# Gates and ups kept by column tile, block products of 256 columns, and the step-size projection in four column groups

## The chip, the cores and the metric

The kernel runs on one core of one Trainium2 chip. TensorE (PE in the profile) multiplies matrices, VectorE (DVE) and ScalarE (ACT) do the elementwise work, GpSimd (POOL) issues a few transfers that add into their destination, and SyncE (SP) issues the other transfers. PEld is TensorE's loading of weights. The metric is the device time of one execution, in microseconds (us), as the median of several runs.

## The reference

The model is an encoder of two layers on one sequence of 512 frames with 1024 channels, in float32. Each layer is a half-weighted SwiGLU, a mixer, and another half-weighted SwiGLU, each on a normalised input and added to x:

```python
def _swiglu(h, w_gate, w_up, w_down):
    return (jax.nn.silu(h @ w_gate) * (h @ w_up)) @ w_down
...
        h = _rmsnorm(x, ffn1_norm[layer])
        x = x + 0.5 * _swiglu(h, ffn1_w_gate[layer], ffn1_w_up[layer], ffn1_w_down[layer])
        h = _rmsnorm(x, mix_norm[layer])
        if layer % 2 == 0:
            proj = h @ even_w_in[i]
            zxbcdt, u = jnp.split(proj, [SSD_INNER + SSD_XBC + SSD_HEADS], axis=-1)
            y_a = _ssd_mixer(zxbcdt, ssd_conv_w[i], ssd_conv_b[i], ssd_dt_bias[i],
                             ssd_a_log[i], ssd_d[i], ssd_norm[i])
...
```

The hidden width of a SwiGLU is 2816, that is 22 column tiles of 128, or 11 pairs of tiles. In the state-space half (SSD) of the even mixer eight columns of the input projection give the step sizes, dt = softplus(dt + dt_bias), and the decay is the running sum of dt * (-exp(a_log)).

## The kernel before

Activations lie transposed: 128 channels on the partitions, 512 frames along the free axis; so a projection of one column tile is a matmul of 512 columns (frames) for each of 8 channel tiles. Float32 is emulated: each operand is split into a rounded high part and a low rest (ScalarE casts the high part, VectorE subtracts to get the low one), and three matmuls (high by high, high by low, low by high) take the place of one. The tiles whl and wh hold split weights, hg split activations, raw weights as they arrive.

The stages follow one another: f0 (a SwiGLU, about 0 to 379 us), the even mixer (to 560), f1 and f2 (to 904 and 1255), the odd mixer (to 1434) and f3. In a SwiGLU the first column pairs are done plainly (8 of 11 in f0, 2 of 11 in f1 to f3, the table CLASSIC): proj_tile() makes one tile, evac() scales it out of PSUM (rsB is the norm's factor, applied late), gate() applies Silu, multiplies gate by up and splits the result into hg. The other column pairs are done by pair() with seven block products in place of eight (a scheme of Strassen's kind, on blocks of 512 channels by 128 columns of weights and 256 frames): feed() builds sums of weight blocks on VectorE, blocks() sums of activation blocks, block() does a product of four 128-channel steps, and plus(), add and times gather the seven results from PSUM on VectorE. pair() leaves its last product to be done in the next one (last, called as before). With WIDE set, the three products that take one of the summed activation tiles (TA, TB) send the high and low halves of the activation through as one matmul of 512 columns, whose two halves of PSUM plus() then adds with two additions; without it they send two matmuls of 256 columns into the same half, and one addition does.

The down-projections (out_unit) run between the pairs, also in plain matmuls of 512 columns. Most raw weights are split by ScalarE and VectorE; those that BY_DMA names are split by split_dma(): ScalarE writes the negated high part and POOL's transfer adds the raw weights from memory to it.

A planner orders the instructions of TensorE, VectorE and ScalarE while the program is built: Clock estimates when each engine and tile is ready, and generators (threads, with priorities PRIO) wait in on() until their inputs will be ready by the main stream's own time plus a margin (SLACK for TensorE; BACKLOG and GUARD bound how far VectorE and ScalarE may be filled ahead). Each engine then runs its list in that order. In the even mixer, ssd_dt() turns the step sizes into dt and the decays, s5_bounce() and s5_eighth() carry the S5 half through memory (us, s5us, s5ys, parameter tiles prm), and ssd_chunk() and ssd_tail() do the SSD half. The transfers of all of these go through SyncE's one queue, in the order in which they are written. The step-size columns are the first projection of the even mixer: proj_tile(wdt, m=8), 24 matmuls whose output is 8 partitions wide. Norm sums (sq, acc, then ones by acc on TensorE) are gathered beside the last down-projections. Nearly every instruction is recorded through one helper, so the profile gives them all one line, 223 (226 in the changed kernel); groups are told apart by tiles.

## Time and profile before

| | |
|---|---|
| median of 3 runs | 1810.75 us (1807.51 to 1813.69) |
| the profiled execution | 1812.46 us, span 1810.8 us |
| TensorE busy | 1787.6 us, 99% of the span, granted clock 0.998 |
| VectorE busy | 1518.0 us, 84% |
| ScalarE busy | 744.5 us, 41% |
| POOL busy | 33.9 us, 2% |
| bytes moved | 216.57 MB, mean 120 GB/s |

A row of a group gives the line, engine, operation, output and inputs by tile name, their shapes and count; then the busy time in us, the mean length of one in ns, and the idle time of the engine just before them with what ended it. A row of a timeline gives start and length in us, the engine and the operation, how many of one kind ran in a row (x), and in brackets the idle time before it and what released it. A row of the chain of waits gives a start and a length on the path that ended last. A row of busy time by stretch gives, after the stretch and its length, the busy us (and instructions) of PE, PEld, DVE, ACT and POOL, then the granted clock of TensorE, the busy share of the DMA engines and GB/s. A row of waits gives the engine and tile that waited, what for, the us in total, how often, and the longest.

### The profile page before, as it was taken

What the parts mean: (1) busy time and instruction counts of PE and PEld (TensorE: products, weight loads), DVE (VectorE), ACT (ScalarE), POOL (GpSimd) and SP (SyncE); (2) the same over time, 40 slices, a digit from 0 to 9 for tenths busy, and PEclk for the clock granted to TensorE, in tenths of its full rate; (3) what the DMA queues carried; (4) which work ended last, traced back from release to release, by engine and by line L of the source; (5) the groups of instructions that cost most, each with busy time, mean ns of one, the idle gap of its engine ahead of it and who ended that gap; (6) DMA issues with size and microseconds to landing.
All of it is one profiled execution on the core that took longest, in us unless ns stands there. A gap on an engine that the chain in (4) does not pass through costs nothing.

```text
span 1810.8 us, 26209 instructions
## 1 busy us (share of the span) xinstructions
PE 1787.6 (99%) x10082; PEld 1536.4 (85%) x10082; DVE 1518.0 (84%) x2902; ACT 744.5 (41%) x1032; POOL 33.9 (2%) x53
## 2 busy tenths in 40 slices
PE   9999999999999999999999999999999999999999
PEld 7876888878778889998888999988888888999987
DVE  8989888778885899998779998987678679998984
ACT  4323433333584543333354333333466554333331
POOL 0000000000010000000010000000000010000000
PEclk9999999999999999999999999999999999999999
DMA  5346533336674533333343333333325452333332
GB/s 193 101 130 173 165 93 94 124 133 197 170 180 131 126 105 105 105 104 106 128 114 107 105 106 105 103 108 116 111 82 114 132 128 86 112 105 95 115 98 77
DMA packets 83341, 216.57 MB, mean 120 GB/s; under 512 B 18288, under 2 KB 30608, under 8 KB 82064
## 3 DMA queue, kind: packets, MB, share of 16 engines
q1 hardware_dynamic: 78032, 196.52, 33.9%
q0 software_dynamic: 5040, 18.35, 5.9%
q8 instruction: 79, 1.29, 0.3%
q14 instruction: 46, 0.38, 0.1%
q10 hardware_dynamic: 144, 0.02, 0.0%
HBM read 202.26 MB, written 12.60 MB: 119 GB/s over the span
## 4 chain that ended last, share of the span: by engine, by line
PE 75%; DVE 15%; DMA 5%; issue 2%; ACT 2%; SPq 1%; DVEq 0%; ACTq 0%
PE ps L223 75%; DVE whl L223 3%; DMA raw<-in_wgu_dram 2%; DVE hg L223 2%; DVE raw L223 2%; DVE us L223 1%; ACT whl L223 1%; DVE gs L223 1%; SPq L223 1%; DVE ct L223 1%; DVE ex L223 1%; DMA prm<-ct 1%; DVE g L223 0%; DMA prm<-prm 0%; DMA raw<-in_wev_dram 0%
## 5 line engine op out<-in xcount | busy, mean ns | idle before, releaser
L223 PE MATMUL ps<-hg,whl 128*128 128x512 f32 (+1 forms) x8400 | 1593.3, 350 | 5.4 <-DVE gs L223 2.5
L223 PEld LDWEIGHTS ps<-hg,whl 128*128 128x128 f32 x8400 | 1341.5, 189 | 210.9 <-issue 7.7
L223 ACT CAST whl<-raw 128x1024 fp32r<-128x1024 f32 x374 | 390.4, 1047 | 437.3 <-PE ps L223 306.6
L223 DVE TENSOR_TENSOR whl<-raw,whl 128x1024 fp32r<-128x1024 f32 x339 | 412.1, 1218 | 81.0 <-ACT whl L223 80.6
L223 ACT CAST hg<-us 128x512 fp32r<-128x512 f32 x88 | 52.7, 618 | 209.0 <-DVE us L223 208.9
L223 DVE TENSOR_TENSOR raw<-raw,raw 128x512 f32<-128x512 f32 (+1 forms) x212 | 131.0, 646 | 2.5
L223 ACT ACTIVATE gs<-gs 128x1024 f32<-128x1024 f32 x44 | 46.7, 1060 | 155.0 <-DVE gs L223 154.9
L223 DVE SCALAR_TENSOR_TENSOR x<-ps,x 128x512 f32<-128x512 f32 x128 | 83.1, 683 | 23.9 <-PE ps L223 23.9
L223 PE MATMUL ps<-hg,wh 128*128 128x512 f32 x480 | 94.2, 339 | 1.1 <-DVE gs L223 1.1
L223 PEld LDWEIGHTS ps<-hg,wh 128*128 128x128 f32 x480 | 77.3, 189 | 13.9 <-DVE gs L223 1.7
L223 DVE TENSOR_TENSOR us<-ps,us 128x256 f32<-128x256 f32 x150 | 63.5, 424 | 22.2 <-PE ps L223 17.8
L223 DVE TENSOR_TENSOR raw<-raw 128x512 f32<-128x512 f32 (+1 forms) x92 | 54.5, 592 | 18.9 <-DMA raw<-in_wgu_dram 18.8
L223 DVE TENSOR_TENSOR gs<-ps,gs 128x256 f32<-128x256 f32 x150 | 63.6, 424 | 6.6 <-PE ps L223 1.0
L223 DVE TENSOR_TENSOR hg<-us,hg 128x512 fp32r<-128x512 f32 x88 | 58.4, 684 | 2.7 <-ACT hg L223 2.7
L223 DVE TENSOR_TENSOR us<-gs,us 128x1024 f32<-128x1024 f32 x44 | 53.7, 1220 | 0.4
L223 DVE TENSOR_TENSOR us<-ps,p 128x256 f32<-128x256 f32 x90 | 37.8, 419 | 16.1 <-PE ps L223 15.4
L223 DVE TENSOR_TENSOR p<-ps,rsB 128x256 f32<-128x256 f32 x120 | 49.9, 416 | 1.7 <-PE ps L223 1.7
L223 ACT ACTIVATE hg<-x,gains 128x512 fp32r<-128x512 f32 x48 | 33.5, 718 | 34.6 <-DVE x L223 32.1
L223 DVE TENSOR_TENSOR gs<-ps,p 128x256 f32<-128x256 f32 x90 | 37.8, 420 | 8.1 <-PE ps L223 6.3
L223 DVE TENSOR_TENSOR wh<-raw,wh 128x512 fp32r<-128x512 f32 x60 | 41.0, 684 | 0.0
L223 ACT ACTIVATE whl<-raw 128x1024 fp32r<-128x1024 f32 x35 | 36.9, 1056 | 8.1 <-PE ps L223 5.1
L223 DVE SCALAR_TENSOR_TENSOR hg<-x,gains,hg 128x512 fp32r<-128x512 f32 x48 | 35.3, 745 | 5.7 <-ACT hg L223 5.7
(258 smaller groups left out, 1084.2 us busy)
## 6 DMA issues: line engine op xcount, KB each, us to landing
raw<-in_wgu_dram SPq DMA_DIRECT2D x176, 512.0 KB, 3.5
raw<-in_wdn_dram SPq DMA_DIRECT2D x88, 512.0 KB, 4.1
whl<-in_wgu_dram POOLq DMA_DIRECT2D x18, 512.0 KB, 6.3
raw<-in_wev_dram SPq DMA_DIRECT2D x16, 512.0 KB, 4.2
prm<-prm SPq DMA_DIRECT2D x8, 1024.0 KB, 6.9
raw<-in_wod_dram SPq DMA_DIRECT2D x12, 512.0 KB, 3.5
raw<-in_wevo_dram SPq DMA_DIRECT2D x8, 512.0 KB, 6.4
raw<-in_wodo_dram SPq DMA_DIRECT2D x8, 512.0 KB, 6.4
```

The costliest lines, as they stand in the source:

```text
L223: r = f(*args, **kw)
```

## The change

The gate and up tiles gs and us become tiles of one column tile (512 frames) in place of two, three of gs and two of us (HALVES); Silu, the multiplication and the split are done for each half as it is ready, in plain and block pairs alike. WIDE is off, so all block products are of 256 columns: 720 matmuls of 512 columns become 1440 of 256, and 180 additions on VectorE go. The step-size projection takes unsplit float32 weights, padded from 8 to 32 columns: four channel tiles go to four groups of 32 output partitions, in two sets of high and low activations (proj_quarters), and a matmul with a stacked identity (sel), in place of a transpose, adds the groups up. The exponential of a_log moves to small(), in f0. BY_DMA gives two in place of three column tiles per gate and up to the accumulating transfers in f1 to f3, so 12 such transfers stay of 18. In the planner the even mixer's BACKLOG goes from 2.5 to 2.0 and its SLACK from 0.0 to 0.5, a matmul of 32 partitions is costed at 0.24, and POOL's transfers in f1 to f3 at a lower rate. One buffer of sq in place of two, and shared tags for two tiles of the S5 preparation, make room.

```diff
 LEAD = (0, 0)
+HALVES = {"gs": 3, "us": 2}
 
-WIDE = (True, True)
+WIDE = (False, False)
 
...
 AHEAD = {"f0": 4, "even": 2, "f1": 4, "f2": 4, "odd": 2, "f3": 4}
-BACKLOG = {"f0": 2.5, "even": 2.5, "f1": 1.5, "f2": 1.5, "odd": 3.0, "f3": 1.5}
+BACKLOG = {"f0": 2.5, "even": 2.0, "f1": 1.5, "f2": 1.5, "odd": 3.0, "f3": 1.5}
 GUARD = {"f0": 2.5, "even": 1.5, "f1": 1.5, "f2": 1.5, "odd": 2.0, "f3": 1.5}
-BY_DMA = {"wgu1": (1, 4), "wgu2": (1, 4), "wgu3": (1, 4), "wev": (13, 16), "wglu": (0, 2), "wevo": (0, 1), "wod": (8, 16), "wodo": (0, 1)}
+BY_DMA = {"wgu1": (2, 4), "wgu2": (2, 4), "wgu3": (2, 4), "wev": (13, 16), "wglu": (0, 2), "wevo": (0, 1), "wod": (8, 16), "wodo": (0, 1)}
 LOADS = (1, 4)
...
 WARM = 12
-SLACK = {"f0": 1.5, "even": 0.0, "f1": 0.0, "f2": 0.0, "odd": 0.4, "f3": 0.0}
+SLACK = {"f0": 1.5, "even": 0.5, "f1": 0.0, "f2": 0.0, "odd": 0.4, "f3": 0.0}
 PREP_SLACK = 4.0
...
                 return (n + 32) / 2400
+            if out.partition_size() == 32 and n == 512:
+                return 0.24
             if out.partition_size() == 64:
...
             self.t["POOL"] = max(at, self.t["POOL"]) + 1.1
-            end = max(self.t["DMA"], self.t["POOL"] + 1.0) + max(0.18, out.free_size() * out.partition_size() * 4 / 360e3)
+            end = max(self.t["DMA"], self.t["POOL"] + 1.0) + max(0.18, out.free_size() * out.partition_size() * 4 / (160e3 if self.ffn else 360e3))
             self.t["DMA"] = end
...
             v.memset(self.inv[:, i:i + 1], 1.0 / (i + 1))
-        self.wdt = c.tile([P, 2, 64], F32R, name="wdt")
-        yield from self.split_steps(wdr, self.wdt)
+        self.sel, self.ea = tile("sel", 8), tile("ea", 8)
+        for i in range(4):
+            yield from self.on("DVE")
+            v.tensor_copy(out=self.sel[32 * i:32 * i + 32], in_=self.ident[32 * i:32 * i + 32, 32 * i:32 * i + 8])
+        yield from self.on("DVE", self.sh8)
+        yield from self.exp_steps(c, self.ea, self.sh8[:, 1], [8])
 
...
 
+
+    def proj_quarters(self, w, h):
+        nc = self.nc
+        ps = self.main_ps()
+        for kk in range(0, KD, 4):
+            for j in range(2):
+                for q in range(4):
+                    k = kk + q
+                    self.until(lambda: h[k] is not None)
+                    nc.tensor.matmul(out=ps[32 * q:32 * q + 32, :], lhsT=w[:, 32 * k:32 * k + 32], rhs=h[k][:, j].bitcast(F32),
+                                     start=kk + j == 0, stop=kk + j == KD - 3)
+                self.tick()
+        return ps
+
     def evac_rs(self, ps, out):
...
                         t = {}
-                    last = self.pair(w, t, "us" if i else "gs", pending)
-
-                    def pending(last=last, t=t, q=q, i=i):
-                        last()
+                    def ready(m, t=t, q=q, i=i):
                         if i == 0:
-                            nc.scalar.activation(out=t["gs"], in_=t["gs"], func=AF.Silu)
+                            nc.scalar.activation(out=t["gs", m], in_=t["gs", m], func=AF.Silu)
                         else:
-                            self.add("gate", self.gate(t, g, q, [1] * 4, 1))
-                            if q == NFF // 2 - 1:
-                                self.give(*self.N, *self.TS)
+                            self.add("gate", self.gate(t, g, q, m, False))
+
+                    last = self.pair(w, t, "us" if i else "gs", pending, ready)
+
+                    def pending(last=last, q=q, i=i):
+                        last()
+                        if (q, i) == (NFF // 2 - 1, 1):
+                            self.give(*self.N, *self.TS)
+
                 else:
...
 
+
     def ftile(self, tag):
-        self.wait_room(tag, 1)
-        return self.ft.tile([P, 2, S], F32, tag=tag, name=self.n(tag), bufs=1)
+        self.wait_room(tag, HALVES[tag])
+        return self.ft.tile([P, S], F32, tag=tag, name=self.n(tag), bufs=HALVES[tag])
 
-    def evac(self, ps, t, tag, m, done):
+    def evac(self, ps, t, tag, m, g, q):
         while not self.scaled():
             yield
-        while t[tag] is None and self.cnt.get(tag, 0):
-            yield
-        if t[tag] is None:
-            self.cnt[tag] = 1
-            t[tag] = self.ft.tile([P, 2, S], F32, tag=tag, name=self.n(tag), bufs=1)
+        yield from self.room(tag, HALVES[tag])
+        o = self.ft.tile([P, S], F32, tag=tag, name=self.n(tag), bufs=HALVES[tag])
         yield from self.on("DVE", ps, self.rsB)
-        self.evac_rs(ps, t[tag][:, m])
+        self.evac_rs(ps, o)
         self.free(ps)
-        done.append(1)
+        t[tag, m] = o
+        if tag == "us":
+            self.add("gate", self.gate(t, g, q, m, True))
 
...
 
-        add(dst[:, 0, hi], Z[:, lo], dst[:, 0, hi])
+        add(d0[:, hi], Z[:, lo], d0[:, hi])
         p5 = new("p5", 1)
         times(p5, Z[:, hi], hi)
-        add(dst[:, 0, hi], dst[:, 0, hi], p5)
+        add(d0[:, hi], d0[:, hi], p5)
         self.block(X, W1, 512, N[4:8], lo, more=True)
         self.give(W1)
-        times(dst[:, 0, lo], X[:, lo], lo)
+        times(d0[:, lo], X[:, lo], lo)
         self.free(X)
+        ready(0)
+        t[tag, 1] = d1 = self.ftile(tag)
         self.block(Y, W4, 0, TB, 0, more=True, wide=wide)
         self.give(W4)
-        plus(dst[:, 1, hi], Y, p1)
-        add(dst[:, 1, hi], Z[:, lo], dst[:, 1, hi])
+        plus(d1[:, hi], Y, p1)
+        add(d1[:, hi], Z[:, lo], d1[:, hi])
         self.free(Z)
...
 
-    def gate(self, t, g, q, ready, done):
+    def gate(self, t, g, q, m, silu):
         nc = self.nc
-        while len(ready) < 4:
-            yield
-        gs, us = t["gs"], t["us"]
-        if done < 1:
+        gs, us = t["gs", m], t["us", m]
+        if silu:
             yield from self.on("ACT", gs)
             nc.scalar.activation(out=gs, in_=gs, func=AF.Silu)
-        if done < 2:
-            yield from self.on("DVE", gs, us)
-            nc.vector.tensor_tensor(out=us, in0=gs, in1=us, op=ALU.mult)
+        yield from self.on("DVE", gs, us)
+        nc.vector.tensor_tensor(out=us, in0=gs, in1=us, op=ALU.mult)
         self.leave("gs")
-        for i in range(2):
-            o = yield from self.grab("hg")
-            yield from self.split_steps(us[:, i], o)
-            g[2 * q + i] = o
+        o = yield from self.grab("hg")
+        yield from self.split_steps(us, o)
+        g[2 * q + m] = o
         self.leave("us")
...
         yield from self.on("DVE", ps8)
-        d8 = self.s5pool.tile([8, S], F32, tag="th", name="d8", bufs=2)
-        v.tensor_tensor(out=d8, in0=ps8[0:8], in1=self.rsB[0:8], op=ALU.mult)
+        d8 = self.s5pool.tile([P, S], F32, tag="th", name="d8", bufs=2)
+        v.tensor_tensor(out=d8, in0=ps8, in1=self.rsB, op=ALU.mult)
         self.free(ps8)
...
         for k in range(4):
-            nc.tensor.transpose(out=pst[:, 8 * k:8 * k + 8], in_=d8[:, k * P:(k + 1) * P], identity=self.ident[0:8, 0:8])
+            nc.tensor.matmul(out=pst[:, 8 * k:8 * k + 8], lhsT=d8[:, k * P:(k + 1) * P], rhs=self.sel, start=True, stop=True)
         self.leave("th")
...
         v.scalar_tensor_tensor(out=self.DT, in0=q, scalar=2.0, in1=x, op0=ALU.mult, op1=ALU.add)
-        ea = p.tile([P, 8], F32, name="ea")
-        yield from self.exp_steps(p, ea, self.sh8[:, 1], [8])
         self.dA = t("dA")
-        v.scalar_tensor_tensor(out=self.dA, in0=self.DT, scalar=-1.0, in1=ea.unsqueeze(1).to_broadcast(sh),
+        v.scalar_tensor_tensor(out=self.dA, in0=self.DT, scalar=-1.0, in1=self.ea.unsqueeze(1).to_broadcast(sh),
                                op0=ALU.mult, op1=ALU.mult)
...
                 if n == 0:
-                    self.add("ssd_dt", self.ssd_dt(self.proj_tile(self.wdt, h, m=8, step=8)))
+                    self.add("ssd_dt", self.ssd_dt(self.proj_quarters(self.wdt, h)))
                 ps = self.proj_tile(w, h)
```

How the orders differ at three places. In these rows ps is a PSUM tile, and the number behind a name tells one tile from another.

TensorE at the start of the even mixer, where wdt holds the step-size weights, ones by acc is the norm's sum, and whl the first full projection. Before:

```order
L223 MATMUL ps_3515<-hg_3492,wdt 8x512 x3
L223 MATMUL ps_3515<-hg_3520,wdt 8x512 x3
L223 MATMUL ps_3561<-ones,acc_3405 128x1 x4
L223 MATMUL ps_3580<-hg_3388,whl_3342 128x512 x3
L223 MATMUL ps_3580<-hg_3403,whl_3342 128x512 x3
L223 MATMUL ps_3580<-hg_3412,whl_3342 128x512 x3
L223 MATMUL ps_3580<-hg_3429,whl_3342 128x512 x3
```

Changed:

```order
L226 MATMUL ps_3636<-hg_3590,wdt 32x512
L226 MATMUL ps_3636<-hg_3600,wdt 32x512
L226 MATMUL ps_3636<-hg_3613,wdt 32x512
L226 MATMUL ps_3636<-hg_3642,wdt 32x512
L226 MATMUL ps_3674<-hg_3504,whl_3497 128x512 x3
L226 MATMUL ps_3674<-hg_3519,whl_3497 128x512 x3
L226 MATMUL ps_3681<-ones,acc_3521 128x1 x4
```

The last set of four step-size matmuls reads the last tile of h (hg_3642, hg_3520 before); two steps of the first projection now stand ahead of the norm's sum, where before they stood behind it.

SyncE's queue in the middle of the even mixer: s5ys and s5us are scratch in memory (stores), prm and raw loads of parameters and weights, yv and hg loads back from scratch. Before:

```order
L223 DMA s5ys_3999<-ys_3942 16x8x64 x8
L223 DMA s5us_3969<-us_3960 128x512
L223 DMA prm_4011<-prm_144 128x2048
L223 DMA prm_4077<-prm_145 128x2048
L223 DMA raw_4082<-in_wev_dram 128x1024
L223 DMA s5ys_4084<-ys_3990 16x8x64 x8
L223 DMA yv_4093<-s5ys_3999 128x512
L223 DMA hg_4101<-s5us_3969 16x16x64 x8
```

Changed:

```order
L226 DMA s5ys_4081<-ys_4058 16x8x64 x8
L226 DMA s5us_4042<-us_4033 128x512
L226 DMA prm_4092<-prm_143 128x2048
L226 DMA prm_4112<-prm_144 128x2048
L226 DMA raw_4139<-in_wev_dram 128x1024
L226 DMA yv_4162<-s5ys_4081 128x512
L226 DMA hg_4168<-s5us_4042 16x16x64 x8
L226 DMA raw_4209<-in_wev_dram 128x1024
L226 DMA prm_4222<-prm_145 128x2048
L226 DMA s5ys_4227<-ys_4110 16x8x64 x8
```

The second group of eight stores to s5ys stood between the store of s5us and the eight loads hg from it; now it stands behind those loads, and one more prm load too.

VectorE in the first block pair of f1: p and gs gather block results from PSUM, us is the multiplication by the up of an earlier pair, hg a split of activations, whl and wh of weights. Before:

```order
L223 TENSOR_TENSOR p_787_5768<-ps_5746,rsB_5469 128x256
L223 TENSOR_TENSOR us_5665<-gs_5624,us_5665 128x1024
L223 TENSOR_TENSOR gs_5772<-ps_5773,p_787_5768 128x256
L223 TENSOR_TENSOR gs_5772<-ps_5773,gs_5772 128x256
L223 TENSOR_TENSOR hg_5771<-us_5665,hg_5771 128x512
L223 TENSOR_TENSOR hg_5799<-us_5665,hg_5799 128x512
L223 TENSOR_TENSOR gs_5772<-ps_5784,gs_5772 128x256
L223 TENSOR_TENSOR p_793_5815<-ps_5784,rsB_5469 128x256
L223 TENSOR_TENSOR gs_5772<-gs_5772,p_793_5815 128x256
L223 TENSOR_TENSOR whl_5821<-raw_5721,whl_5821 128x1024
L223 TENSOR_TENSOR wh_795_5827<-raw_5676,wh_795_5827 128x512
L223 TENSOR_TENSOR gs_5772<-ps_5746,rsB_5469 128x256
```

Changed:

```order
L226 TENSOR_TENSOR p_814_5864<-ps_5844,rsB_5559 128x256
L226 TENSOR_TENSOR us_5850<-gs_5809,us_5850 128x512
L226 TENSOR_TENSOR hg_5843<-raw_5784,hg_5843 128x2x256
L226 TENSOR_TENSOR gs_5866<-ps_5867,p_814_5864 128x256
L226 TENSOR_TENSOR hg_5875<-us_5850,hg_5875 128x512
L226 TENSOR_TENSOR gs_5866<-ps_5884,gs_5866 128x256
L226 TENSOR_TENSOR p_819_5912<-ps_5884,rsB_5559 128x256
L226 TENSOR_TENSOR gs_5866<-gs_5866,p_819_5912 128x256
L226 TENSOR_TENSOR whl_5918<-raw_5793,whl_5918 128x1024
L226 TENSOR_TENSOR wh_823_5928<-raw_5765,wh_823_5928 128x512
L226 TENSOR_TENSOR gs_5866<-ps_5844,rsB_5559 128x256
```

From the first scaled copy p to the gs that frees its bank, one addition to gs and one of two activation splits went (another split, of a summed activation, came in), and the multiplication of 1024 columns is one of 512.

More of the change, by code (lines that the diff above doesn't have):

```diff
@@ L117, in __init__ @@
         self.w, self.r, self.floor, self.stuck = {}, {}, 0.0, 0
-        self.reads, self.writes, self.fine = {}, {}, True
+        self.reads, self.writes, self.fine, self.ffn = {}, {}, True, False
         self.lanes, self.born = [0.0] * 8, {}
@@ L297, in phase @@
         self.name = name
-        self.clk.fine = name == "f0"
+        self.clk.fine, self.clk.ffn = name == "f0", name in ("f1", "f2", "f3")
         self.backlog, self.guard, self.most = BACKLOG[name], GUARD[name], AHEAD[name]
@@ L469, in small @@
         self.cvw, self.sh8, self.ssv, self.hb = tile("cvw", 8, 5), tile("sh8", 2, 8), tile("ssv", 8), tile("hb", 4)
-        self.psc, wdr, gq = tile("psc", 4), tile("wdr", 64), tile("gq", 2)
+        self.psc, self.wdt, gq = tile("psc", 4), tile("wdt", KD * 32), tile("gq", 2)
         for t, nm in ((self.cvw, "cvw"), (self.sh8, "ssdh"), (self.ssv, "ssv"), (self.hb, "bglu"), (self.psc, "poolsc"),
-                      (wdr, "wdt"), (gq, "qkg")):
+                      (self.wdt, "wdt"), (gq, "qkg")):
             nc.sync.dma_start(out=t, in_=A[nm])
@@ L663, in norm_factors @@
             else:
-                sq = self.rsp.tile([P, S], F32, tag="sq", name=self.n("sq"), bufs=2)
+                sq = self.rsp.tile([P, S], F32, tag="sq", name=self.n("sq"), bufs=1)
                 nc.scalar.activation(out=sq, in_=x, func=AF.Square)
@@ L804, in ffn @@
                     if (m % 2, i) == (0, 0):
-                        t, done = {"gs": None, "us": None}, []
+                        t = {}
                     if (m, i) == (0, 0):
@@ L813, in ffn @@
                         self.give(w)
-                    self.add("evac", self.evac(ps, t, "us" if i else "gs", m % 2, done))
-                    if (m % 2, i) == (1, 1):
-                        self.add("gate", self.gate(t, g, m // 2, done, 0))
-                        if m == NFF - 1:
-                            self.give(*h)
+                    self.add("evac", self.evac(ps, t, "us" if i else "gs", m % 2, g, m // 2))
+                    if (m, i) == (NFF - 1, 1):
+                        self.give(*h)
                 elif key[0] == "pair":
@@ L822, in ffn @@
                         t = {}
[L823 to L832 removed]
+                    def ready(m, t=t, q=q, i=i):
+                        if i == 0:
+                            nc.scalar.activation(out=t["gs", m], in_=t["gs", m], func=AF.Silu)
+                        else:
+                            self.add("gate", self.gate(t, g, q, m, False))
+                    last = self.pair(w, t, "us" if i else "gs", pending, ready)
+                    def pending(last=last, q=q, i=i):
+                        last()
+                        if (q, i) == (NFF // 2 - 1, 1):
+                            self.give(*self.N, *self.TS)
                 else:
@@ L940, in block, with pair @@
             self.tick()
-    def pair(self, w, t, tag, before):
+    def pair(self, w, t, tag, before, ready):
         v = self.nc.vector
@@ L966, in pair @@
             before()
-        t[tag] = dst = self.ftile(tag)
+        t[tag, 0] = d0 = self.ftile(tag)
         Y = self.main_ps()
         self.block(Y, W3, 512, TA, 1, wide=wide)
-        plus(dst[:, 0, hi], Y, p1)
+        plus(d0[:, hi], Y, p1)
         if not before:
@@ L993, in last @@
             self.give(W2)
-            plus(dst[:, 1, lo], Y, p1)
+            plus(d1[:, lo], Y, p1)
             self.free(Y)
+            ready(1)
         return last
-    def gate(self, t, g, q, ready, done):
+    def gate(self, t, g, q, m, silu):
         nc = self.nc
-        while len(ready) < 4:
-            yield
-        gs, us = t["gs"], t["us"]
-        if done < 1:
+        gs, us = t["gs", m], t["us", m]
+        if silu:
             yield from self.on("ACT", gs)
             nc.scalar.activation(out=gs, in_=gs, func=AF.Silu)
-        if done < 2:
-            yield from self.on("DVE", gs, us)
-            nc.vector.tensor_tensor(out=us, in0=gs, in1=us, op=ALU.mult)
+        yield from self.on("DVE", gs, us)
+        nc.vector.tensor_tensor(out=us, in0=gs, in1=us, op=ALU.mult)
         self.leave("gs")
-        for i in range(2):
-            o = yield from self.grab("hg")
-            yield from self.split_steps(us[:, i], o)
-            g[2 * q + i] = o
+        o = yield from self.grab("hg")
+        yield from self.split_steps(us, o)
+        g[2 * q + m] = o
         self.leave("us")
@@ L1155, in s5_prepare @@
         brr, bri = bc4[:, 0], bc4[:, 1]
-        bmx, t16, t17 = tl("s5bm", [G + 1, 16]), tl("s5t16", [G, 16]), tl("s5t17", [G, 16])
+        bmx = tl("s5bm", [G + 1, 16])
+        t16, t17 = (pool.tile([P, G, 16], F32, tag=tag, name=self.n("t")) for tag in ("s5bt", "s5tc"))
         v.memset(bmx[:, G:G + 1], 0.0)
@@ L2072, in layout @@
     A["wev"] = _tiles(we, [c for _, _, c in EVEN_ORDER])
-    A["wdt"] = we[:, DT_COL:DT_COL + 8].reshape(KD, P, 8).transpose(1, 0, 2).reshape(P, 64)
+    wdt = np.zeros((P, KD, 32), np.float32)
+    wdt[:, :, 0:8] = we[:, DT_COL:DT_COL + 8].reshape(KD, P, 8).transpose(1, 0, 2)
+    A["wdt"] = wdt.reshape(P, KD * 32)
     A["wevo"] = _stream(i["even_w_out"][0])
```

2 lines of the change are left out of this document (removed).

## The prediction

> **What bounds the kernel now.** I read the page first, then the busy time by stage, then the chain of waits in order of time, and last the timeline where that chain leaves TensorE. From the page, parts 1 and 4:
>
> ```profile
> span 1810.8 us, 26209 instructions
> PE 1787.6 (99%) x10082; PEld 1536.4 (85%) x10082; DVE 1518.0 (84%) x2902; ACT 744.5 (41%) x1032; POOL 33.9 (2%) x53
> PE 75%; DVE 15%; DMA 5%; issue 2%; ACT 2%; SPq 1%; DVEq 0%; ACTq 0%
> ```
>
> Busy time of each engine in four of six stretches (f0, even mixer, f1, f3):
>
> ```profile
> 0.00:375.00 375.00, 368.25 (x1846) 306.69 (x1847) 320.11 (x697) 135.36 (x189) 0.74 (x6) 1.00 0.43 131
> 375.00:560.00 185.00, 176.27 (x1041) 142.46 (x1040) 148.88 (x371) 91.50 (x153) 7.77 (x9) 0.98 0.63 180
> 560.00:904.00 344.00, 342.83 (x2016) 304.08 (x2015) 299.66 (x505) 138.87 (x166) 5.10 (x6) 1.00 0.36 110
> 1434.00:1811.00 377.00, 371.69 (x2143) 327.41 (x2141) 314.05 (x526) 141.20 (x169) 5.11 (x6) 1.00 0.34 104
> ```
>
> TensorE lacks 6.8 us in f0, 8.7 in the even mixer, 1.2 in f1, 5.3 in f3, which holds the end. So two things can move the time: the length of the matmul stream, and about 20 us of gaps. VectorE is busy for 84% of the span, yet the chain of waits runs through one unbroken piece of TensorE in each stage of column pairs (f1 and f3 shown):
>
> ```profile
> 453.36 3.75 DMA hg<-s5us
> 470.64 9.01 DMA prm<-prm
> 641.36 301.29 PE ps L223 x1797
> 1517.22 289.57 PE ps L223 x1736
> ```
>
> Time taken from VectorE inside such a piece buys nothing.
>
> **The blocks of 256 columns.** 720 matmuls of 512 columns become 1440 of 256. Their pace is in TensorE's timeline: a projection in 512 columns, then one whole column pair of f1 (with a down-projection unit in it), then a run of 256 columns:
>
> ```profile
> 373.64 5.83 PE L223 MATMUL ps<-hg,whl 128*128 128x512 f32 x25
> 710.63 1.56 PE L223 MATMUL ps<-hg,wh 128*128 128x512 f32 x8
> 712.03 14.24 PE L223 MATMUL ps<-hg,whl 128*128 128x256 f32 x88
> 726.10 1.56 PE L223 MATMUL ps<-hg,wh 128*128 128x512 f32 x8
> 714.88 1.73 PE L223 MATMUL ps<-hg,whl 128*128 128x256 f32 x13
> L223 PE MATMUL ps<-hg,whl 128*128 128x512 f32 x5040 | 1250.8, 394 | 3.0 <-DVE hg L223 1.6 <-DVE whl L223 1.0 <-ACT whl L223 0.3
> L223 PE MATMUL ps<-hg,whl 128*128 128x256 f32 x3360 | 489.8, 283 | 2.4 <-DVE gs L223 2.4
> L223 DVE TENSOR_TENSOR gs<-ps,gs 128x256 f32<-128x256 f32 x150 | 63.6, 424 | 6.6 <-PE ps L223 1.0
> ```
>
> A run ends with one matmul's own length, 0.394 us (512 columns) or 0.283 (256), so the pace is (5.83 - 0.394)/24 = 0.2265 us and (1.73 - 0.283)/12 = 0.1206. From 710.63 to 726.10 are 15.47 us for 24 plain matmuls of 512, 48 narrow ones and 12 wide pieces (one of 512 and one of 256): 15.47 - 24 x 0.2265 - 48 x 0.1206 = 4.25, or 0.354 per wide piece. The three narrow matmuls in its place cost 3 x 0.1206 = 0.362: 8 ns more, 720 times, +5.8 us. Bounds: nothing, if only columns count (768 either way, and half of 0.2265 is 0.113); +8.5 us from the first four wide pieces alone, (712.03 - 710.63)/4 = 0.350. Each nanosecond of the 0.1206, read off a run of 13, moves the answer by 7 x 720 ns = 5 us, so I lean a little from 5.8 towards the lower bound and take **+5**.
>
> The Trainium skill ("TensorE: Matmul & The Clock Gate", section Back-to-back issue gap) speaks against this part of the change as well: it gives 262 cycles for 256 columns and 518 for 512, so a split pays 6 cycles. By that, an estimate from its figures, the 720 extra matmuls cost 1.8 us at its 2.4 GHz, and the total would be 3 us lower; the trace's own paces are longer than both of its figures.
>
> With the wide pieces go 180 VectorE additions, 90 to a gate and 90 to an up: 180 x 0.424 = 76 us. Inside the pairs they lie beside TensorE's unbroken pieces: 0.
>
> **Halves.** VectorE's 44 multiplications of 1024 columns become 88 of 512, ScalarE's Silu likewise. The nearest rows:
>
> ```profile
> L223 DVE TENSOR_TENSOR us<-gs,us 128x1024 f32<-128x1024 f32 x44 | 53.7, 1220 | 0.4
> L223 DVE TENSOR_TENSOR hg<-us,hg 128x512 fp32r<-128x512 f32 x88 | 58.4, 684 | 2.7 <-ACT hg L223 2.7
> L223 ACT ACTIVATE gs<-gs 128x1024 f32<-128x1024 f32 x44 | 46.7, 1060 | 155.0 <-DVE gs L223 154.9
> L223 DVE TENSOR_TENSOR whl<-raw,whl 128x1024 fp32r<-128x1024 f32 x339 | 412.1, 1218 | 81.0 <-ACT whl L223 80.6
> ```
>
> VectorE +44 x (2 x 0.684 - 1.220) = +6.5 us; ScalarE at most +44 x (2 x 0.684 - 1.060) = +13.6. Six weight units go from POOL's accumulating transfer to VectorE, 6 x 1.22 = +7.3 us, and ScalarE loses a pass for each. The planner's longer estimate for POOL's transfers moves splits only. All of it is covered by the 76 us given back and by a ScalarE at 41%: 0. Uncovered, at the front of a pair, one split would cost its 1.2 us once in each of three stages.
>
> **Where VectorE did hold TensorE.** The first pair of f1, f2 and f3: the waits grouped, VectorE's busy time just ahead, and TensorE's row in f1:
>
> ```profile
> PE ps L223 <- DVE gs L223: 3.6, 7, 0.9
> 626.00:632.00 6.00, 6.00 (x39) 5.39 (x38) 5.96 (x9) 2.76 (x3) 0.00 (x0) 1.00 0.15 29
> 639.34 1.67 PE L223 MATMUL ps<-hg,whl 128*128 128x256 f32 x12 [0.81 <-DVE gs L223]
> ```
>
> VectorE is full there. Between the scaled copy and the result that frees the bank (its rows are shown with the change) the new order has one addition of 0.42 us fewer and a multiplication shorter by 1.22 - 0.68 = 0.54: 0.96 us of the 3.6/3 = 1.2 that each stage waits, 2.9 in all. Its bounds are the whole 3.6 us, and nothing, if weight splits slide into the place. I take **-3**.
>
> **The step-size projection.** TensorE, VectorE and the nearest rows for a plain fp32 matmul and for column groups:
>
> ```profile
> 379.30 5.70 PE L223 MATMUL ps<-hg,wdt 128*8 128x512 f32 x24
> 383.51 0.75 DVE L223 SCALAR_TENSOR_TENSOR hg<-x,gains,hg 128x512 fp32r<-128x512 f32 x1
> 384.31 0.15 PEld L223 LDWEIGHTS ps<-hg,wdt 128*8 128x8 f32 x2 [0.30 <-DVE hg L223]
> 384.91 1.05 PE L223 MATMUL ps<-ones,acc 128*128 128x1 f32 x8
> 125.15 0.42 PE L223 MATMUL ps<-g,s5bm 128*32 128x128 f32 x8 [1.29 <-ACT bl L223]
> L223 PE MATMUL ps<-plo,pw 128*128 128x512 f32 x8 | 4.2, 602 | 0.0
> ```
>
> The last row is of four fp32 matmuls of 512 columns, two records each: 4.2/4 = 1.05 us for one alone, which is a pace and a last record of 0.602, so the pace is 0.45 per record and 0.90 per matmul (bounds 0.602 and 1.05). The eight rows at 125.15, four groups of 32 columns, lie inside 0.42 us, so groups run together. Sixteen matmuls in four sets cost 4 x 0.90 = 3.6 us against 384.91 - 379.30 = 5.6. But the fourth set reads the low half of the last tile, which VectorE ends at 383.51 + 0.75 = 384.26, and VectorE's order there is unchanged. The set ends near 384.26 + 0.05 + 0.90 = 385.2 (the 0.05 as at 384.31), where 384.9 stood before. The 2.0 us saved are waited away: **+0.3** (bounds -2 and +0.5). One square buffer in place of two holds back a square by under 0.7 us, behind six projections of 0.2265 that now stand ahead of the sums: 0.
>
> **The even mixer's order.** TensorE's long waits, and SyncE's queue between them:
>
> ```profile
> 406.17 0.38 PE L223 MATMUL ps<-dA,tri 128*128 128x32 f32 x2 [0.88 <-DVE cr L223]
> 457.35 0.96 PE L223 MATMUL ps<-hg,prm 128*64 128x64 f32 x18 [2.03 <-DMA hg<-s5us]
> 479.78 0.69 PE L223 MATMUL ps<-hg,prm 128*64 128x64 f32 x16 [2.30 <-DMA prm<-prm]
> 534.61 1.66 PE L223 MATMUL ps<-hg,whl 128*128 128x512 f32 x6 [1.17 <-DVE hg L223]
> 541.28 1.05 PE L223 MATMUL ps<-ones,ysq 128*128 128x1 f32 x8 [1.15 <-DVE ysq L223]
> 440.64 8.62 SPq L223 DMA_DIRECT2D s5ys<-ys  x8
> 449.78 4.02 SPq L223 DMA_DIRECT2D hg<-s5us  x8
> L223 DVE SCALAR_TENSOR_TENSOR ex<-ex,ex 128x32 f32<-128x32 f32 x24 | 4.6, 192 | 0.8
> ```
>
> The eight gathers at 449.78 stood behind eight stores that held the queue for 8.62 us. In the new order those stores come later, so the gathers issue some 5 us earlier while their reader moves up by 18 matmuls (18 x 0.2265 = 4.1 us): the 2.03 goes. The last parameter load, issued at 470.64, takes 9.01 us and is read at 479.78 after 2.30 of waiting; in the new order 33 matmuls (7.5 us) and some 1.5 us of side work lie between issue and reader: about 0.5 of the wait stays. The two waits at the tail keep about 2.1 of 2.32, because the last state-space chunk moves 21 matmuls back. The matmul at 406 moves up by 9 (2.0 us) and the chain before it loses an exponential of 16 small steps (16 x 0.19 = 3.1 us, now done in f0); but the wait is on VectorE's queue (cr), where other steps slide up, so I keep 1.2 for its 0.88. Sum -2.0 - 1.8 - 0.2 + 0.3 = -3.7, taken as **-4** (bounds -7.5, all five gone, and +4).
>
> **Sum.** +5 - 3 + 0.3 - 4 = -1.7; f0's side work and the odd mixer, whose TensorE order is unchanged, 0 +- 3. The profiled execution took 1812.46 us around a span of 1810.8, 1.7 above the median of 1810.75. From it the sum gives 1810.8, from the median 1809.0. I say **1809**, since the time is compared with the median.
>
> **Rivals.**
> *Gaps close fully.* The even waits go (-7.5), the pairs' too (-3.6), and the narrow blocks cost +2, with +0.3 for the projection: -8.8, near 1802. For it: VectorE, 84% busy, ends most of the short waits, and SyncE's queue is the long one. Against: each moved reader moves up with its data.
> *Column groups run one after another.* Then 16 x 0.90 = 14.4 us stand where 5.6 stood, all on TensorE ahead of everything in the even mixer: +8.8 in place of +0.3, and the total is 1809 + 8.5 = 1817.5. It decides from about 1.7 us per set upward, where three sets no longer end by 384.3: (384.3 - 379.3)/3. Against it the eight rows in 0.42 us, which are of 128 columns, not 512.
> *Only the longer stream arrives.* The new order opens a wait for each it closes (0 in place of -7): 1810.75 + 5.3 = 1816. The tail speaks for it: VectorE is nearly full there, and the matmuls that covered the last chunk are 21 fewer.
>
> **How the numbers follow.** A measurement tells about 0.3%, 5.4 us, from no change: below 1805.3 is faster, above 1816.2 slower. My forecast has 0.47, gaps closing fully 0.35, groups in turn 0.08, only the longer stream 0.10. The forecast's own range is 1804 to 1813. The first rival lies almost wholly in faster, the second in slower, the third half in slower; a little of the forecast lies on each side: faster 0.36, same 0.49, slower 0.15. For 8 in 10 the range goes from 1800, inside the first rival, to 1818, past the second and third.
>
> **What would show it.** Narrow blocks: a pair's period with its unit near 15.56 us in place of 15.47. The transitions: the grouped wait of TensorE on gs below 1 us. Projection: sixteen matmuls ending within 0.5 us of VectorE's last low half. Queue: no wait of TensorE on hg<-s5us, and under 1 us on the last prm. I am wrong if a pair keeps its period, if the sixteen matmuls take over 6 us, or if the even mixer is not 3 to 5 us shorter.

## The result, and the profile after

The changed kernel takes 1828.93 us (median of 6 runs, 1824.31 to 1832.32) against 1810.26 us (6 runs, 1807.51 to 1813.69): a ratio of 1.0098, with a 95% interval of 1.0078 to 1.0118. It is 1% slower. The forecast was 1809 us with a range to 1818, and none of its rivals had the cause.

The page of the changed kernel, parts 1, 4 and 5, first. Its profiled execution took 1824.37 us, span 1822.6, granted clock 0.996:

```profile
span 1822.6 us, 27512 instructions
PE 1795.0 (98%) x10814; PEld 1574.9 (86%) x10814; DVE 1454.9 (80%) x2775; ACT 751.1 (41%) x1069; POOL 28.8 (2%) x47
PE 82%; DVE 11%; issue 3%; ACT 2%; DMA 2%; SPq 0%; DVEq 0%; ACTq 0%; POOLq 0%
L226 ACT ACTIVATE sq<-x 128x512 f32<-128x512 f32 x42 | 26.3, 625 | 30.3 <-DVE acc L226 30.2
```

VectorE was relieved as computed (1518.0 to 1454.9 us), and TensorE's busy time grew by 7.4 us. The new thing is the last row: ScalarE's squares (sq) spent 30 us waiting for VectorE's additions (acc). The waits, grouped, of the kernel before and then of the changed one:

```profile
ACT sq L223 <- DVE acc L223: 2.5, 2, 2.1
PE ps L223 <- DVE gs L223: 3.6, 7, 0.9
```

```profile
ACT sq L226 <- DVE acc L226: 30.2, 24, 2.6
PE ps L226 <- DVE acc L226: 6.7, 4, 2.6
PE ps L226 <- DVE s_sc L226: 3.3, 2, 2.9
PE ps L226 <- DVE gs L226: 0.4, 1, 0.4
```

Two of these rows are news: TensorE waits 6.7 us for acc, a wait that the kernel before doesn't have, and 2.9 us at once for s_sc in the even mixer. The wait on gs, which the prediction meant to remove, is gone (3.6 to 0.4). The six norm sums (TensorE's matmuls ones by acc) are good landmarks. In the changed kernel:

```profile
25.15 1.05 PE L226 MATMUL ps<-ones,acc 128*128 128x1 f32 x8 [0.64 <-DVE acc L226]
390.55 0.95 PE L226 MATMUL ps<-ones,acc 128*128 128x1 f32 x8
595.54 1.02 PE L226 MATMUL ps<-ones,acc 128*128 128x1 f32 x8 [2.63 <-DVE acc L226]
945.94 1.05 PE L226 MATMUL ps<-ones,acc 128*128 128x1 f32 x8 [0.84 <-DVE acc L226]
1291.72 1.05 PE L226 MATMUL ps<-ones,acc 128*128 128x1 f32 x8
1478.15 1.02 PE L226 MATMUL ps<-ones,acc 128*128 128x1 f32 x8 [2.63 <-DVE acc L226]
```

Distances between these landmarks in us, with two kernels of the experiments below; the last column goes to TensorE's last instruction:

| kernel (profiled execution) | start to f0's sum | to even | to f1 | to f2 | to odd | to f3 | to the end |
|---|---|---|---|---|---|---|---|
| before | 21.2 | 363.7 | 205.5 | 347.6 | 346.3 | 182.1 | 340.4 |
| changed | 25.1 | 365.4 | 205.0 | 350.4 | 345.8 | 186.4 | 340.5 |
| changed, two square buffers | 21.1 | 365.0 | 204.9 | 347.9 | 345.5 | 182.3 | 340.5 |
| before, one square buffer | 25.2 | 364.1 | 206.3 | 349.4 | 346.3 | 184.1 | 340.9 |

In the two forms of the changed kernel six projections (6 x 0.2265 = 1.4 us) stand ahead of the even mixer's sum, so "to even" is longer and "to f1" shorter by 1.4 us than the work itself. Counted from the start of the step-size projection, f0's part after its sum is as long as before (358.0 us against 358.1), and the even mixer takes 212.4 us against 211.1 (212.3 with two square buffers). The changed kernel thus loses 3.9 us before the first sum, 1.3 in the even mixer, 2.8 in f1's stretch and 4.3 in the odd mixer's. Of the 2.8, 0.8 is the wait in front of f2's sum; of the 4.3, 2.6 is the wait in front of f3's. The rest of these two is mostly clock, as shown below. How a norm becomes late shows in the timeline around f1's sum, first before (the last square, its addition, the sum), then changed:

```profile
588.94 0.62 ACT L223 ACTIVATE sq<-x 128x512 f32<-128x512 f32 x1
589.60 0.69 DVE L223 TENSOR_TENSOR acc<-acc,sq 128x512 f32<-128x512 f32 x1 [1.67 <-ACT sq L223]
590.38 1.02 PE L223 MATMUL ps<-ones,acc 128*128 128x1 f32 x8
```

```profile
588.28 0.63 ACT L226 ACTIVATE sq<-x 128x512 f32<-128x512 f32 x1 [1.23 <-DVE acc L226]
588.82 1.04 ACT L226 CAST whl<-raw 128x1024 fp32r<-128x1024 f32 x1
589.76 0.72 ACT L226 ACTIVATE hg<-x,gains 128x512 fp32r<-128x512 f32 x1
...
592.60 0.74 DVE L226 SCALAR_TENSOR_TENSOR hg<-x,gains,hg 128x512 fp32r<-128x512 f32 x1
593.26 0.68 DVE L226 TENSOR_TENSOR acc<-acc,sq 128x512 f32<-128x512 f32 x1
594.04 0.63 ACT L226 ACTIVATE sq<-x 128x512 f32<-128x512 f32 x1 [0.72 <-DVE acc L226]
594.70 0.69 DVE L226 TENSOR_TENSOR acc<-acc,sq 128x512 f32<-128x512 f32 x1 [0.76 <-ACT sq L226]
595.54 1.02 PE L226 MATMUL ps<-ones,acc 128*128 128x1 f32 x8 [2.63 <-DVE acc L226]
```

With one buffer a square can't start until the addition of the square before it is done. That addition stands in VectorE's list behind weight splits and low halves, and what stands behind the square in ScalarE's list (casts of weights, the high half of the next tile) waits with it. The two engines' lists, which were written for two buffers, turn into one chain, and TensorE waits 2.63 us at its end.

A second loss lies in the clock. Busy time by stretch of the changed kernel, on both sides of that wait, and inside the second stretch:

```profile
589.00:595.50 6.50, 3.91 (x18) 2.90 (x16) 4.41 (x5) 4.94 (x6) 0.86 (x1) 1.00 0.21 23
595.50:602.00 6.50, 6.46 (x30) 5.52 (x31) 1.79 (x11) 0.04 (x1) 0.00 (x0) 0.74 0.31 61
596.70:599.90 3.20, 3.20 (x9) 2.49 (x8) 1.68 (x11) 0.00 (x0) 0.00 (x0) 0.50 0.24 47
```

Behind the wait the granted clock is 0.74 over 6.5 us, that is 2 x 0.26 x 6.5 = 3.4 us at half, and 1.7 us lost if TensorE's work takes twice as long there; inside, it reads 0.50. That is most of the rest of the 2.8 us in f1's stretch. The rest of the 4.3 us in the odd mixer's is another such piece, at 1303 us, which has no wait of over 0.3 us in the 7 us before it, so it can't be put down to a norm. Over all runs, (1 - granted clock) x span is on average 9.7 us for the changed kernel (mean clock 0.9947) and 2.3 us for the kernel before (0.9987, 21 runs taken later). So by this estimate some 7 of the 18.7 us are clock; the other 11 are the later start, waits and extra matmuls, less what was saved. The profiled execution, 11.8 us longer in span than the one before, had one of the better clocks of the six.

### The profile page after: what moved, and what is told of

Read it like the earlier page. It is cut to its first block, busy times and chain, and to the rows that moved or that the text cites. A ratio compares the mean times of both kernels' runs of the same rounds, so it can differ in the third digit from the quotient of the medians.

```text
span 1822.6 us, 27512 instructions
## 1 busy us (share of the span) xinstructions
PE 1795.0 (98%) x10814; PEld 1574.9 (86%) x10814; DVE 1454.9 (80%) x2775; ACT 751.1 (41%) x1069; POOL 28.8 (2%) x47
## 4 chain that ended last, share of the span: by engine, by line
PE 82%; DVE 11%; issue 3%; ACT 2%; DMA 2%; SPq 0%; DVEq 0%; ACTq 0%; POOLq 0%
PE ps L226 82%; DVE whl L226 2%; DVE raw L226 2%; DVE hg L226 2%; ACT whl L226 1%; DVE acc L226 1%; DVE us L226 1%; DVE x L226 1%; DVE gs L226 0%; DVE s_t L226 0%; ACT hg L226 0%; DVE ex L226 0%; DMA whl<-in_wglu_dram 0%; DMA prm<-prm 0%; ACT sq L226 0%
## 5 line engine op out<-in xcount | busy, mean ns | idle before, releaser
L226 PE MATMUL ps<-hg,whl 128*128 128x256 f32 (+1 forms) x8880 | 1599.1, 340 | 6.5 <-DVE hg L226 1.8
L226 PEld LDWEIGHTS ps<-hg,whl 128*128 128x128 f32 x8880 | 1367.4, 190 | 187.9 <-issue 5.6
L226 DVE TENSOR_TENSOR whl<-raw,whl 128x1024 fp32r<-128x1024 f32 x345 | 419.0, 1218 | 129.3 <-ACT whl L226 129.1
L226 ACT ACTIVATE gs<-gs 128x512 f32<-128x512 f32 x88 | 55.5, 631 | 169.5 <-DVE gs L226 169.5
L226 PEld LDWEIGHTS ps<-hg,wh 128*128 128x128 f32 x720 | 93.9, 191 | 4.4
L226 PE MATMUL ps<-hg,wh 128*128 128x256 f32 x720 | 96.0, 283 | 0.0
L226 DVE TENSOR_TENSOR us<-gs,us 128x512 f32<-128x512 f32 x88 | 60.1, 683 | 4.1 <-ACT gs L226 3.6
L226 DVE TENSOR_TENSOR us<-ps,us 128x256 f32<-128x256 f32 x60 | 25.4, 424 | 36.2 <-PE ps L226 34.9
L226 ACT ACTIVATE sq<-x 128x512 f32<-128x512 f32 x42 | 26.3, 625 | 30.3 <-DVE acc L226 30.2
L226 ACT CAST wh<-raw 128x512 fp32r<-128x512 f32 x60 | 36.9, 615 | 0.0
```

Source lines behind the costliest of these rows:

```text
L226: r = f(*args, **kw)
```

## The experiments

Three theories: S, the single square buffer; N, the 720 extra matmuls; O, the new order of the even mixer. Later C: a wait of TensorE costs more than itself, through the clock.

**One square buffer in the kernel before**

```diff
-                sq = self.rsp.tile([P, S], F32, tag="sq", name=self.n("sq"), bufs=2)
+                sq = self.rsp.tile([P, S], F32, tag="sq", name=self.n("sq"), bufs=1)
```

> The kernel before with one buffer for the squares (sq) in place of two, and nothing else; the lists of TensorE, VectorE and ScalarE stay word for word the same. Theory S (the single square buffer is the cause): the sums of squares come late at the six norms, TensorE waits for acc as in the changed kernel (6.7 us there in 4 waits, plus a start that is 3.9 us later), so 8 to 16 us slower than before, 1818 to 1826. Rival N (the 720 extra matmuls are the cause) and rival O (the new order of the even mixer is): no change, 1808 to 1813, and no wait of TensorE on acc over 0.7 us.

Measured: 1821.86 us (5 runs), 1.0058 (1.0046 to 1.0071) of before: +10.6 us from changing one number. The last row of the table shows the same places, and the waits name it:

```profile
ACT sq L223 <- DVE acc L223: 24.9, 22, 2.6
PE ps L223 <- DVE acc L223: 4.2, 3, 1.8
```

N and O, which have no part in this kernel, fall as sole causes.

**Two square buffers in the changed kernel**

```diff
-HALVES = {"gs": 3, "us": 2}
+HALVES = {"gs": 2, "us": 2}
...
-                sq = self.rsp.tile([P, S], F32, tag="sq", name=self.n("sq"), bufs=1)
+                sq = self.rsp.tile([P, S], F32, tag="sq", name=self.n("sq"), bufs=2)
```

> The changed kernel with two square buffers again, paid for by two gs buffers in place of three; the lists of TensorE, VectorE and ScalarE stay the same as in the changed kernel. Theory S: the waits on acc go, 10 to 18 us faster than the changed kernel, 1808 to 1816, and the clock granted in the profile comes back to about 0.998. Rivals N and O: it stays within 4 us of the changed kernel, 1825 to 1833; it is slower still if the third gs buffer carried something.

Measured: 1812.65 us (11 runs), 1.0014 (1.0004 to 1.0023) of before. 16.3 us come back, the table's stretches are those of before within 1.3 us (the largest difference, "to even", is the six projections), and TensorE waits for acc no more. Two edits were made at once, since the memory has no room for three gs buffers and two of squares; the control takes the first alone:

**Two gs buffers, still one of squares**

```diff
-HALVES = {"gs": 3, "us": 2}
+HALVES = {"gs": 2, "us": 2}
```

> The changed kernel with two gs buffers in place of three and still one square buffer; all orders as in the changed kernel. It tells the two edits of the earlier run apart. Theory S: nothing changes, 1825 to 1833. If the third gs buffer, not the second square buffer, made the difference: about 1812.

Measured: 1829.20 us (4 runs), 1.0101 (1.0084 to 1.0117). So the third gs buffer shows no gain, and the second square buffer alone is worth the 16.6 us between this kernel and the one above.

**Wide blocks in the changed kernel**

```diff
-WIDE = (False, False)
+WIDE = (True, True)
```

> The changed kernel with the wide blocks of 512 columns again (and with them the 180 additions). Theory N: 5 to 9 us faster than the changed kernel, 1820 to 1824. Theory S: the loss stays where it was, at the norms, and only the price of the narrow blocks comes back, 0 to 5 us, 1824 to 1829; the additions may lengthen the waits of the first pairs again by up to 3.6 us.

Measured: 1824.35 us (4 runs), 1.0075 (1.0061 to 1.0089); the loss stays at the norms (2.63 us of waiting for acc in front of f1 and of f3, as in the changed kernel). The difference of 4.6 us to the changed kernel is loose, since the two kernels' runs spread over 4 and 8 us, and it lies on the border of what N and S gave. The same edit without the norms' noise:

**Wide blocks, with two square buffers**

```diff
-HALVES = {"gs": 3, "us": 2}
+HALVES = {"gs": 2, "us": 2}
-WIDE = (False, False)
+WIDE = (True, True)
...
-                sq = self.rsp.tile([P, S], F32, tag="sq", name=self.n("sq"), bufs=1)
+                sq = self.rsp.tile([P, S], F32, tag="sq", name=self.n("sq"), bufs=2)
```

> The changed kernel with two square buffers (and two of gs), and with the wide blocks again: halves, step-size projection, even mixer's order and transfers as changed. If the narrow blocks cost 3 to 5 us: 1808 to 1810 against 1812.6 with them. If they cost nothing, or if the 180 additions make the pairs' front wait again: 1811 to 1814.

Measured: 1810.33 us (11 runs), 1.0000 (0.9991 to 1.0009): 2.3 us less than with narrow blocks. From sum to sum f1, f2 and f3 take 346.0, 345.2 and 340.1 us against 347.9, 345.5 and 340.5, that is 2.6 us less, although TensorE sits idle for 1.1 us more in the wide form at the fronts of the pairs of f1 and f3. So the 720 extra matmuls cost about 4 us of TensorE, and 2 to 3 net.

**Narrow blocks alone, in the kernel before**

```diff
-WIDE = (True, True)
+WIDE = (False, False)
```

> The kernel before with WIDE off alone: 720 matmuls of 512 columns in pairs of 256, 180 additions fewer. By the prediction's terms +5 for the matmuls and, at the front of the pairs, up to -2 for the additions: 1813 to 1816. If only the square buffer mattered: 1809 to 1813, and the runs of TensorE in f1, f2 and f3 keep their length to 1 us.

Measured: 1822.51 us (5 runs), 1.0070 (1.0057 to 1.0082): +11.7 us, over twice what either view allowed. TensorE's own pace is the usual one; the waits on gs grew from 3.6 to 8.3 us:

```profile
PE ps L223 <- DVE gs L223: 8.3, 8, 1.9
655.72 1.22 DVE L223 TENSOR_TENSOR whl<-raw,whl 128x1024 fp32r<-128x1024 f32 x1
656.86 1.22 DVE L223 TENSOR_TENSOR us<-gs,us 128x1024 f32<-128x1024 f32 x1
658.18 0.42 DVE L223 TENSOR_TENSOR gs<-ps,p 128x256 f32<-128x256 f32 x1
658.66 2.63 PE L223 MATMUL ps<-hg,whl 128*128 128x256 f32 x16 [1.70 <-DVE gs L223]
```

With 180 additions gone the planner put other work into VectorE's list, here a weight split, ahead of the multiplication that frees the one gs tile of 1024 columns; the next result waits behind both. The rest, some 3 us beside the 4 of the matmuls and 4.7 of these waits, may be clock (mean 0.9972 against 0.9987, 5.1 us against 2.3); that was not taken apart.

**The SwiGLU part as a whole, in the kernel before**: halves (two gs, two us), narrow blocks, fewer accumulating transfers; the rest as before. Beside the changed evac(), gate(), pair() and the planner's rate for POOL's transfers:

```diff
+HALVES = {"gs": 2, "us": 2}
-WIDE = (True, True)
+WIDE = (False, False)
-BY_DMA = {"wgu1": (1, 4), "wgu2": (1, 4), "wgu3": (1, 4),
+BY_DMA = {"wgu1": (2, 4), "wgu2": (2, 4), "wgu3": (2, 4),
```

> The kernel before with the half tiles (two gs, two us), the narrow blocks and the fewer accumulating transfers; the step-size projection, the even mixer's order and the two square buffers as before. By the terms: -3 for the fronts of the pairs, +3 to +5 for the narrow blocks, so 1810 to 1813; TensorE's waits on gs are gone. If the even mixer's part of the change was what kept the changed kernel from gaining, this is faster than before: below 1809.

Measured: 1810.69 us (11 runs), 1.0000 (0.9991 to 1.0009). No wait on gs is left in its list of waits. With tiles of half the size the result of the next pair no longer waits for a multiplication of 1024 columns, and the price of the narrow blocks is given back: with the halves they cost nothing that shows here, without them 11.7 us. The fewer accumulating transfers came in with the halves, and their share was not tested alone.

**The even mixer's margins alone, in the kernel before**

```diff
-BACKLOG = {"f0": 2.5, "even": 2.5, "f1": 1.5, "f2": 1.5, "odd": 3.0, "f3": 1.5}
+BACKLOG = {"f0": 2.5, "even": 2.0, "f1": 1.5, "f2": 1.5, "odd": 3.0, "f3": 1.5}
-SLACK = {"f0": 1.5, "even": 0.0, "f1": 0.0, "f2": 0.0, "odd": 0.4, "f3": 0.0}
+SLACK = {"f0": 1.5, "even": 0.5, "f1": 0.0, "f2": 0.0, "odd": 0.4, "f3": 0.0}
```

> The kernel before with the even mixer's SLACK of 0.5 and BACKLOG of 2.0 alone, so only the order of the even mixer moves. By the prediction: its waits fall by about 4 us, 1804 to 1809. Rival O (the order opens as many waits as it closes, or more): 1810 to 1816. Theory S says nothing of it beyond that no wait on acc appears.

Measured: 1812.56 us (11 runs), 1.0006 (0.9996 to 1.0015): no gain. Its long waits on TensorE:

```profile
417.05 1.62 PE L223 MATMUL ps<-hg,prm 128*64 128x64 f32 x48 [1.78 <-DMA hg<-s5us]
534.39 2.93 PE L223 MATMUL ps<-hg,whl 128*128 128x512 f32 x6 [3.54 <-ACT gl L223]
```

The waits at 457 and 480 us are gone, a load of us is waited for earlier, and the tail's two waits became one of 3.54 us: between the sums TensorE sits idle for 7.4 us where 8.7 stood. From the start of the step-size projection to f1's sum the even mixer is 1.1 us shorter in the profiled run (209.9 against 211.1), but the whole kernel isn't, with a mean clock of 0.9977 against 0.9987.

**Matmuls in the wait** (theory C), in the changed kernel with two square buffers:

```diff
+            if e == 5 and i == 0:
+                for _ in range(12):
+                    nc.tensor.eng.matmul(out=psY[:, 256:384], lhsT=self.ones, rhs=self.ones, start=True, stop=True)
```

> The changed kernel with two square buffers (and two of gs), and with twelve small matmuls of ones that nobody reads put into TensorE's 2.9 us wait at 470 us; all other orders stay. Theory C (TensorE's clock is halved for 3.4 us or more after such a wait, so a wait costs more than itself): the stretch of half clock at 471.8 (10.2 us long in the profile) is gone, 2 to 5 us faster, 1807.5 to 1810.5. Rival: the half clock comes by itself, whatever TensorE waits: it stays or moves, 1811 to 1814.

TensorE around the wait in the kernel without them, and the busy time of the 12 us from there:

```profile
470.40 0.43 PE L226 MATMUL ps<-s_sc,prm 128*128 128x63 f32 x2 [2.91 <-DVE s_sc L226]
470.00:482.00 12.00, 11.60 (x63) 10.48 (x64) 11.21 (x30) 2.79 (x6) 0.55 (x1) 0.57 0.65 153
```

and with them:

```profile
469.25 2.84 PE L1352 MATMUL ps<-ones 128*128 128x128 f32 x24
472.42 0.43 PE L226 MATMUL ps<-s_sc,prm 128*128 128x63 f32 x2 [0.16 <-DVE s_sc L226]
470.00:482.00 12.00, 11.46 (x94) 10.23 (x94) 11.53 (x31) 6.24 (x10) 1.15 (x2) 1.00 0.73 185
```

The clock of 0.57 (10.3 us at half) is gone there, and over eleven runs each the mean clock rose from 0.9972 to 0.9987, 2.8 us by (1 - clock) x span. The time fell by 1.6 us, to 1811.05 (1.0008, 0.9999 to 1.0016; by the ratios the fall is 1.1 us), while the two intervals overlap. By its time alone it lies in the rival's range: C is borne out by the clock here, its price only roughly. The Trainium skill ("TensorE: Matmul & The Clock Gate", section HAM oscillation) has the clock fall after idle gaps of over about 3.4 us; here waits of 2.6 and 2.9 us were followed by a lower clock.

**The best parts together, and the same filling there**: the kernel before with halves (two gs, two us) and fewer accumulating transfers, wide blocks; then with ten matmuls of ones ahead of the fifth of the eight S5 steps. The first is the kernel with the SwiGLU part and

```diff
-WIDE = (False, False)
+WIDE = (True, True)
```

The second has in addition

```diff
+        if e == 4:
+            for _ in range(10):
+                nc.tensor.eng.matmul(out=psS[:, 256:384], lhsT=self.ones, rhs=self.ones, start=True, stop=True)
```

> The kernel before with the half tiles (two gs, two us) and the fewer accumulating transfers only: wide blocks, step-size projection, even mixer's order and two square buffers as before. From the stretches between norms with and without narrow blocks (f1 347.6 before, 346.0 with halves and wide blocks; f2 346.3 and 345.2; f3 340.4 and 340.1): 3 us faster than before, 1807 to 1809. If the shorter waits are paid for elsewhere: 1810 to 1812.

> The same with ten small matmuls of ones that nobody reads in TensorE's wait of about 2.4 us for the loads of us in the even mixer (at 458 us); all other orders the same. Theory C (a wait of 2 us and more can halve TensorE's clock for 3.4 us): 1 to 3 us faster than without them, 1805 to 1808, with no stretch of half clock at 458 to 462. Rival: no gain, or the ten matmuls outlast the wait and cost up to 1 us.

Measured: 1808.57 us (11 runs), 0.9993 (0.9984 to 1.0002) of before, and 1809.91 (0.9996, 0.9987 to 1.0005) with the filling. The first beats the changed kernel by 20 us, and lies 1.5 us below before, which its interval doesn't tell from nothing. The filling had little to remove: the wait of 2.4 us that it was meant for was seen in the kernel with the SwiGLU part, and in the profiled run of this one it is 1.0 us, with no lowered clock anywhere (mean clock of all runs 0.9981 and, filled, 0.9982). So this pair of runs says little about C.

## Why the prediction was wrong

**The square buffer, 0 us: the step that failed.** The prediction gave the edit a cost of 0 for two reasons, both taken at one of six norms, the even mixer's: a square is held back "by under 0.7 us", about one addition, and six matmuls now stand ahead of the sum. The first was wrong even there:

```profile
378.15 0.63 ACT L226 ACTIVATE sq<-x 128x512 f32<-128x512 f32 x1 [2.61 <-DVE acc L226]
```

What a square waits for is not the length of an addition but VectorE's coming to that addition in its list: up to 2.6 us, 24 times in all. At that norm the cover held (no wait at 390.55). At the start of the program and in front of f1, f2 and f3 TensorE waits, 6.7 us in all. In the order of before the edit costs 10.6 us, in the changed order 16.3 (1828.9 to 1812.65). Why it is dearer there is shown in part: the waits on acc are longer (6.7 against 4.2 us), and the clock lower (0.9947 against 0.9970).

**The narrow blocks, +5.** Right: about 4 us. The prediction's own sign was the period of a pair with its unit, 15.56 us in place of 15.47. In the changed kernel:

```profile
701.30 1.59 PE L226 MATMUL ps<-hg,wh 128*128 128x256 f32 x12
702.73 14.27 PE L226 MATMUL ps<-hg,whl 128*128 128x256 f32 x96
716.84 1.59 PE L226 MATMUL ps<-hg,wh 128*128 128x256 f32 x12
```

From 701.30 to 716.84 are 15.54 us, 0.07 more; a period has 12 of the 720 matmuls, so 60 x 0.07 = 4.2 us. The estimate of 1.8 us from the Trainium skill ("TensorE: Matmul & The Clock Gate", section Back-to-back issue gap) is too low for this stream.

**The fronts of the pairs, -3.** Right in the changed kernel (3.6 to 0.4 us of waits), but mostly by the halves and not by the fewer additions. In the kernel with halves, fewer accumulating transfers and wide blocks, where no addition goes, these waits are 1.2 us; without halves, fewer additions made them worse (8.3 us), by the mechanism that the prediction had as its bound ("if weight splits slide into the place").

**The step-size projection, +0.3.** Right. In the changed kernel with two square buffers:

```profile
378.69 3.90 PE L226 MATMUL ps<-hg,wdt 128*32 128x512 f32 x30
382.81 0.74 DVE L226 SCALAR_TENSOR_TENSOR hg<-x,gains,hg 128x512 fp32r<-128x512 f32 x1
383.61 1.05 PE L226 MATMUL ps<-hg,wdt 128*32 128x512 f32 x2 [1.02 <-DVE hg L226]
386.08 0.95 PE L226 MATMUL ps<-ones,acc 128*128 128x1 f32 x8
```

Fifteen matmuls take 3.90 us, so the four groups run together and the rival of groups in turn is out. The last one waits 1.02 us for VectorE's last low half (382.81 + 0.74 = 383.55) and ends at 384.66, 1.1 us after it, where 0.95 was forecast (the prediction's sign, "within 0.5 us", didn't fit its own sum). From the first one's start to the last one's end are 5.97 us against 5.70 before, +0.3: the saving is waited away.

**The even mixer's order, -4.** Wrong by about 5, and the second step that failed. The loads of us and of prm were in time, as forecast, and neither wait is left in the changed kernel (with two gs buffers and the same lists, a load of us is waited for again, for 2.2 us). But the second load of y (yv), issued at 454.34 before, now goes out behind eight stores and two loads of weights. ScalarE waits for it, and VectorE for ScalarE, ahead of the steps for s_sc (the first row before, the others changed):

```profile
454.34 1.10 SPq L223 DMA_DIRECT2D yv<-s5ys  x1
454.36 6.16 SPq L226 DMA_DIRECT2D s5ys<-ys  x8
460.62 6.78 SPq L226 DMA_DIRECT2D raw<-in_wev_dram  x2
467.62 0.33 SPq L226 DMA_DIRECT2D yv<-s5ys  x1
471.54 0.63 ACT L226 ACTIVATE g<-yv 128x512 f32<-128x512 f32 x1 [6.12 <-DMA yv<-s5ys]
472.20 0.69 DVE L226 SCALAR_TENSOR_TENSOR g<-g,yv 128x512 f32<-128x512 f32 x1 [3.26 <-ACT g L226]
475.02 1.21 DVE L226 TENSOR_TENSOR s_sc<-s_t,s_t 64x128 f32<-64x128 f32 x4
475.66 0.43 PE L226 MATMUL ps<-s_sc,prm 128*128 128x63 f32 x2 [2.91 <-DVE s_sc L226]
```

TensorE waits 2.91 us for s_sc. With two square buffers the even mixer takes 212.3 us against 211.1 from the start of the projection to f1's sum: 1.2 longer, 0.3 of it the projection, so +0.9 in place of -4. TensorE's idle time outside the projection did fall by 2.1 us (8.7 to 6.7), but the stretch at half clock around the s_sc wait (10.2 us, against 6.8 in the even mixer before) took 1.7 of it back. The prediction had the sign for this ("if the even mixer is not 3 to 5 us shorter").

**The sum.** Without the cost of the square buffer the terms come to 4 - 3.2 + 0.3 + 0.9 = +2.0 in place of -1.7; measured with two square buffers, 1812.65 - 1811.25 = +1.4. That lies inside the stated range, though by luck of its width: the even mixer's term is wrong in it all the same. Of the rivals, the gaps did not close fully (the even mixer's did not), and the groups did not run in turn, though that rival is nearest in time (1817.5). The third, that the new order opens a wait for each it closes, is right of the even mixer and wrong of the pairs; its 1816 does not hold the square buffer either.
